# A fourth PSUM bank for the scores, and the attention outputs in halves of one bank

## The chip, the cores and the metric

The kernel runs on one core of a Trainium2 chip. The metric is the device time of one execution in microseconds (us). Engines are named as the profile names them: PE is TensorE (matmuls), PEld its weight loads, DVE is VectorE, ACT is ScalarE, POOL is GpSimd, and SP issues most DMAs. PSUM is the memory that PE writes its products to; here it is eight banks of 512 fp32 values in each of 128 partitions.

## The reference, cut to what matters

One layer with two attention branches over a prompt of 2048 frames (16 tiles of 128), and over 8 running streams of 16 frames each (one tile more, called the sample).

```python
h, gate = adaln_modulate(xp, c_prompt, norm_g[l], w_ada[l], b_ada[l])
qa, ka, va, za, qb, kb, vb, zb, ga, gb = project_inputs(h, w_in[l], pos_p)

def diff_attention(q, k, v, qpos, kpos, lam):          # branch a, 4 heads, each with two scores
    s = einsum('bqhcd,bkhcd->bhcqk', q, k) * HEAD_DIM_A ** -0.5
    p = softmax(where(mask, s, -inf), axis=-1)
    w = p[:, :, 0] - lam * p[:, :, 1]
    return einsum('bhqk,bkhe->bqhe', w, v)

def stick_breaking_attention(q, k, v, qpos, kpos):     # branch b, 8 heads
    z = einsum('bqhd,bkhd->bhqk', q, k) * HEAD_DIM_B ** -0.5
    log_1m = where(mask, log_sigmoid(-z), 0.0)
    log_a = log_sigmoid(z) + cumsum(log_1m, axis=3, reverse=True) - log_1m
    return einsum('bhqk,bkhd->bqhd', where(mask, exp(log_a), 0.0), v)

ya = (rms_norm(oa, subln_g) * (1 - lam_init) * silu(za)) @ w_branch_a
yb = (ob * silu(zb)) @ w_branch_b
xp = xp + gate * ((sigmoid(ga) * ya + sigmoid(gb) * yb) @ w_out)
```

The sample goes through the same with a cache of 512 older keys and values. Outputs are the normed results and the new keys and values.

## The kernel before, in words

There are three phases. In the first, the input is normed and modulated (`modulated`), tile group by tile group, and written as two fp16 halves (high and low part) to DRAM. The second is the longest: eight units, one after the other. An even unit (kind 0) is one head of the differential attention, an odd unit (kind 1) two heads of the stick-breaking attention. For each of its 17 tiles a unit projects queries, keys, values and gates (`project`, L452 for the main columns, L528 for gate columns, odd units only), transposes queries and keys (`transpose_qk`), forms scores (`scores`, L681 to L685), turns them into weights and multiplies these with the values (`pv_block`, L738 to L743). In the third phase the branch products (L1428) and the output product (L1457) run tile by tile, with the sample's attention beside them.

The way of one tile through the attention: a chunk of 512 scores is written to a bank called `s`. In an even unit DVE moves it out (L582), and the softmax follows later in pieces that are put off (`later_on`). In an odd unit ACT writes a sigmoid of it to SBUF and another one in place (both L128), and DVE then runs a product scan over the bank (L658); only after that scan is the bank free. POOL multiplies scan and sigmoid (L664). In both, the weights are cut into two fp16 halves (`turn`, L596, L597), transposed by a DMA (L604) into one of five buffers `wt`, and multiplied with the values by PE into a bank `o`. Tiles of more than 8 blocks of keys have two such segments for a head. After the last product of a tile its output is evicted (`natural`): by ACT alone in an even unit (L717), by ACT and then DVE in an odd one (L722, L723), with a product on POOL (L725); then it is stored (L732).

The eight banks of PSUM are given to four uses, for the whole kernel:

```python
BANKS = {"mm": 2, "s": 3, "t": 1, "o": 2}
```

`mm` takes projections and branch products, `t` transposes and gate columns, `s` scores, transposes of the last phase and small sums, `o` the attention's outputs and the last phase's output product. In the first phase `modulated` alternates between `s` and `o`.

The order of work is made in two steps. The program writes pieces of projection and of scores interleaved by their cost, and counts the cost in `spent`. Work that is put off lies in the list `due`, sorted by the value of `spent` at which it may go; the products of a segment are put there 27 units behind the transposing DMA (`PV_LAG`), and `give` takes everything out that is due. From this order a planner then fixes each engine's own order of instructions, with the waits that the use of tiles demands: an engine takes a later instruction where the planner holds an earlier one not to be ready.

Of the kernel before, what the change touches and what calls it, by code (L numbers as in the profile page):

```python
# [17 lines left out]
F32 = mybir.dt.float32  # L18
# [6 lines left out]
NOSYNC = mybir.DependencyInfo(mybir.DependencyClass.NoSync, mybir.DependencyReason.DATA)  # L25

P = 128
# [6 lines left out]
NT = SEQ // P  # L34
# [84 lines left out]
def layer_kernel(ctx: ExitStack, tc: tile.TileContext, a: dict):  # L119
# [61 lines left out]
    keys_d = {(n, h, i): dram.tile([P, 16, P], F16, name=f"keys_{n}{h}{i}") for n in ("ak", "bk") for h in range(4) for i in range(4)}  # L181

    con = ctx.enter_context(tc.tile_pool(name="con", bufs=1))
    ps = ctx.enter_context(tc.tile_pool(name="ps", bufs=2, space=bass.MemoryType.PSUM))
    tiny = ctx.enter_context(tc.tile_pool(name="tiny", bufs=6))
    unit = ctx.enter_context(tc.tile_pool(name="unit", bufs=2))
    c01 = ctx.enter_context(ExitStack())
# [8 lines left out]
    kvp = c01.enter_context(tc.tile_pool(name="kvp", bufs=2))  # L196
    stg = c01.enter_context(tc.tile_pool(name="stg", bufs=2))

    BANKS = {"mm": 2, "s": 3, "t": 1, "o": 2}

    def bank(tag, dt=F32):
        return ps.tile([P, 512 if dt == F32 else 1024], dt, tag=tag, name=f"ps_{tag}", bufs=BANKS[tag])


    ident = con.tile([P, P], F32, name="ident")
# [383 lines left out]
    def turn(job, seg, scale=None):  # L589

        nb = seg["hi"] - seg["lo"]
        nk = nb * P
        w16 = seg["n"].bitcast(F16)
        hi, lo, src = w16[:, 0:nk], w16[:, nk : 2 * nk], seg["p"][:, 0:nk]
        if scale is None:
            S.copy(out=hi, in_=src)  # L596
            V.tensor_tensor(out=lo, in0=src, in1=hi, op=ALU.subtract)  # L597
        else:
            split(hi, lo, src, scale, S)
        if job["t"] == NT:  # L600
            seg["wt"] = job["pool"].tile([P, 10, P], F16, tag="dwt", name="dwt", bufs=2)
        else:
            seg["wt"] = wtp.tile([P, 2 * SEG, P], F16, tag="wt", name="wt", bufs=WT_BUFS)
        nc.sync.dma_start_transpose(out=seg["wt"][:, 0 : 2 * nb, :], in_=w16[:, 0 : 2 * nk])  # L604
        if job["t"] < NT:
            cost = (PV_A, PV_B)[job["U"]["kind"]]
            for fn in pv(job, seg):
                later_on(PV_LAG, fn, cost)

    def softmax_pair(job):  # L610

# [55 lines left out]
    def scores(U, t, jobs):  # L667

        sc, kind = U["sc"], U["kind"]
        nch = t // 4 + 1  # L670
        own = [new_job(U, t, c, t + 1) for c in range(1 + kind)]
        jobs += own

        def chunk(c, ch):
            job = own[c if kind == 1 else 0]
            seg = job["segs"][ch * 4 // SEG]
            n = 512 if ch < t // 4 else (t % 4 + 1) * P
            p = bank("s")
            qst, kk = U["q", t], U["k"][ch]
            diag = ch == t // 4  # L680
            T.matmul(p[:, 0:n], qst[:, c, :], kk[:, c, 0:n], start=True, stop=False)  # L681
            T.matmul(p[:, 0:n], qst[:, 2 + c, :], kk[:, c, 0:n], start=False, stop=not diag)  # L682
            if diag:
                m = mask_a if kind == 0 else mask_b
                T.matmul(p[:, n - m.shape[1] : n], idb, m, start=False, stop=True)  # L685
            evacuate(job, seg, c, p, ch * 512 - seg["lo"] * P, n, sc[:, 3:4], sc[:, 4:5], ch)
            if kind == 0:
                if diag and c == 1:
                    softmax_pair(job)
                return  # L690
            i = job["segs"].index(seg)
            later = job["segs"][i + 1] if i + 1 < len(job["segs"]) else None
            stick(seg, later, ch * 512 - seg["lo"] * P, n, p)
            if ch * 4 == seg["lo"]:
                if later is not None:
                    stick_weights(job, later, None)
                if i == 0:
                    stick_weights(job, seg, later)

        def silu():  # L700

            z = silu_z[t % len(rings)]
            sg = stg.tile([P, 256], F32, tag="r2", name="r2", bufs=1)[:, 0:P]
            act(out=sg, in_=z, func=AF.Sigmoid)
            V.tensor_tensor(out=z, in0=z, in1=sg, op=ALU.mult)

        order = [(c, ch) for ch in range(nch) for c in range(2)] if kind == 0 else \
                [(c, ch) for c in range(2) for ch in reversed(range(nch))]
        return ([(0.1, silu)] if kind == 1 else []) + [(2.0 if ch < t // 4 else (t % 4 + 1) / 2, lambda c=c, ch=ch: chunk(c, ch)) for c, ch in order]
# [24 lines left out]
    def pv_block(job, seg, po, wj, vt, first, last):  # L734

        wt, nb, c = seg["wt"], seg["hi"] - seg["lo"], job["c"]
        if job["U"]["kind"] == 0:
            T.matmul(po[:, 0:P], wt[:, wj, :], vt[:, :, 0, :], start=first, stop=False)  # L738
            T.matmul(po[:, 0:P], wt[:, wj, :], vt[:, :, 1, :], start=False, stop=False)
            T.matmul(po[:, 0:P], wt[:, nb + wj, :], vt[:, :, 0, :], start=False, stop=last)  # L740
        else:
            T.matmul(po[:, c * P : (c + 1) * P], wt[:, wj, :], vt[:, c, :, :], start=first, stop=False)  # L742
            T.matmul(po[:, c * P : c * P + 64], wt[:, nb + wj, :], vt[:, c, 0, :], start=False, stop=last)  # L743

    due, spent = [], [0.0, 0]

    def later_on(lag, fn, cost=0.0):

        spent[1] += 1
        bisect.insort(due, (spent[0] + lag, spent[1], cost, fn))  # L750

    def pv(job, seg):

# [15 lines left out]
    def give(order, costs):  # L769

        for i, weight, fn in order:
            fn()
            spent[0] += weight * costs[i]
            while due and due[0][0] <= spent[0]:
                _, _, cost, product = due.pop(0)
                product()
                spent[0] += cost

    def cache_column(name, h):
        return "ab".index(name[0]) * 4 + h  # L780
# [231 lines left out]
    with tc.tile_pool(name="p0", bufs=1) as p0:  # L1012
# [160 lines left out]
        def modulated(g):  # L1173

            t0, w = GROUPS[g]
            nt = w // P
            box = {}

            def piece(k):
                if k == 0:  # L1180
                    box["hp"] = hp = hp_tile(F16)[:, 0 : nt * 2 * D].rearrange("p (i a k n) -> p i a k n", a=2, k=KT, n=P)
                    at_hand.update({t0 // P + i: hp[:, i, :, :, :] for i in range(nt)})
                hp = box["hp"]
                pt = bank("so"[k % 2])
                for i in range(nt):
                    T.matmul(pt[:, i * P : (i + 1) * P], xs[g][i][:, k * P : (k + 1) * P], diags[g][:, i, :], start=True, stop=True)
                tmp = p0.tile([P, 512], F32, tag="tmp", name="tmp", bufs=2)
                hi, lo = hp[:, :, 0, k, :], hp[:, :, 1, k, :]
                pv = pt[:, 0:w].rearrange("p (i n) -> p i n", n=P)
                tv = tmp[:, 0:w].rearrange("p (i n) -> p i n", n=P)  # L1190
                if t0 < SEQ:
                    S.activation(out=hi, in_=pv, func=AF.Identity, scale=ab[:, 0, k, 0:1], bias=ab[:, 1, k, 0:1])

                    S.activation(out=tv, in_=hi, func=AF.Identity, bias=minus_b[:, k : k + 1])
                    V.scalar_tensor_tensor(out=lo, in0=pv, scalar=ab[:, 0, k, 0:1], in1=tv, op0=ALU.mult, op1=ALU.subtract)
                else:
                    tb = tmp[:, 0:w].rearrange("p (b s) -> p b s", b=NB)
                    V.tensor_tensor(out=tb, in0=pt[:, 0:w].rearrange("p (b s) -> p b s", b=NB),
                                    in1=ab[:, 0, k, 1:9].unsqueeze(2).to_broadcast([P, NB, NS]), op=ALU.mult)
                    V.tensor_tensor(out=tb, in0=tb, in1=ab[:, 1, k, 1:9].unsqueeze(2).to_broadcast([P, NB, NS]), op=ALU.add)  # L1200
                    S.copy(out=hi, in_=tv)
                    G.tensor_tensor(out=lo, in0=tv, in1=hi, op=ALU.subtract)
                if k == KT - 1:
                    load(out=hT_d[g], in_=hp)

            return [(1.0, lambda k=k: piece(k)) for k in range(KT)]
# [144 lines left out]
    for n in range(len(steps) + 2):  # L1351
# [19 lines left out]
        if at[0] == len(line) and not pieces and not spare and not cached:  # L1371
            if cuts is None:
                cuts = early_work()
            pieces = [(1.0, fn) for fn in cuts[: -(-len(cuts) // (len(steps) + 2 - n))]]
            del cuts[: len(pieces)]
            if n == len(steps) + 1:
                while due and due[0][2] == 0.0:
                    due.pop(0)[3]()
                pieces += [(PV_B / PIECE, fn) for _, _, _, fn in due]
                due.clear()  # L1380
        give(interleaved(pieces, qk, side), (PIECE, CHUNK, 0.0))
    for _, _, _, fn in due:
        fn()
    c01.close()


    with ExitStack() as c2:
# [155 lines left out]
```

## Time and profile before

| | |
|---|---|
| median of 3 runs | 2275.9 us (2274.01 to 2279.74) |
| the profiled execution | 2280.78 us, span 2279.0 us |
| PE busy | 2086.9 us, 92% of the span |
| DVE busy | 1716.8 us, 75% |
| ACT busy | 1617.6 us, 71% |
| POOL busy | 701.4 us, 31% |
| mean granted clock of PE | 0.97 |

The span is the time from the first to the last instruction. The first phase ends near 140 us, the units' scores run from 140 to 1778 us, and the last phase follows. A row such as "PE ps_s L681 <- DVE sc_n L658: 31.3, 29, 3.0" says that PE's instructions of line 681, which write a bank `s`, waited 31.3 us in all for DVE's line 658, 29 times, 3.0 us at the longest. In a timeline a row gives start, duration, engine, line, operation and operands.

### The profile page before, as it was taken

The page shows a single profiled execution, that of the slowest core. Times are in us where ns is not written, and L with a number is a line of the kernel's source. Part 1 is how long each engine was busy: PE and PEld are TensorE (multiplying, and loading weights), DVE is VectorE, ACT ScalarE, POOL GpSimd, SP SyncE. Part 2 cuts the span into 40 slices and gives each one's busy share as a digit, 9 for nine tenths or more (in the row PEclk, how much of TensorE's full clock was granted, in tenths as well). Part 3 has the DMA queues.
Part 4 walks back from the last instruction along what each step waited for, and adds up shares of the span by engine and source line. Part 5 has one row for each costly group of instructions (what it writes and reads, how often), then busy time and mean ns, then how long its engine had stood idle before and what let it go on. Part 6 is the DMA issues. An engine that isn't in the chain of part 4 may idle for free. (4 is left out here: it accounts for less than half of the span.)

```text
span 2279.0 us, 41771 instructions
## 1 busy us (share of the span) xinstructions
PE 2086.9 (92%) x14752; PEld 1122.3 (49%) x14752; DVE 1716.8 (75%) x3795; ACT 1617.6 (71%) x3228; POOL 701.4 (31%) x610
## 2 busy tenths in 40 slices
PE   5998899999999899899999989998997789899998
PEld 3654455554555455455554545554553444444443
DVE  4658768778886787988688788877778777767753
ACT  3967777888887687888677788866778566556541
POOL 1223014446411444642044355302335212211211
PEclk8999999999999999999999999999998799999999
DMA  9777658998796999978888899655677899888321
GB/s 329 271 234 186 160 134 213 197 222 193 201 244 155 221 210 196 211 195 215 193 213 204 200 217 230 172 130 138 153 156 155 203 292 239 221 214 224 122 106 47
DMA packets 805827, 445.30 MB, mean 195 GB/s; under 512 B 537354, under 2 KB 744506, under 8 KB 805104
## 3 DMA queue, kind: packets, MB, share of 16 engines
q1 hardware_dynamic: 804668, 442.24, 78.5%
q8 instruction: 115, 1.88, 0.3%
q14 instruction: 96, 0.79, 0.1%
q10 hardware_dynamic: 948, 0.39, 0.1%
HBM read 228.82 MB, written 86.02 MB: 138 GB/s over the span
## 5 line engine op out<-in xcount | busy, mean ns | idle before, releaser
L664 POOL TENSOR_TENSOR sc_p<-sc_p,sc_n 128x127 f32<-128x127 f32 (+7 forms) x192 | 319.2, 1664 | 701.7 <-DVE sc_n L658 529.6
L452 PEld LDWEIGHTS <-hs 128*128 128x128 f16 x3120 | 293.4, 99 | 332.4 <-DMA hs<-hT_d 15.5
L452 PE MATMUL ps_mm<-wa,hs 128*128 128x512 f16 x1590 | 389.8, 384 | 9.5 <-DMA hs<-hT_d 8.6
L452 PE MATMUL ps_mm<-wb,hs 128*128 128x512 f16 x1530 | 376.9, 381 | 5.8 <-DMA hs<-hT_d 4.8
L528 PE MATMUL ps_t<-wb,hs 128*128 128x512 f16 x1224 | 290.7, 380 | 1.3 <-DVE qst L556 1.0
L658 DVE TENSOR_TENSOR_SCAN sc_n<-ps_s,sc_n,zero_t 128x512 f32<-128x512 f32 x192 | 245.4, 1278 | 48.9 <-ACT ps_s L128 44.2
L681 PE MATMUL ps_s<-k,qst 128*128 128x512 f16 (+3 forms) x640 | 226.0, 354 | 46.3 <-DVE sc_n L658 31.3
L597 DVE TENSOR_TENSOR sc_n<-sc_p,sc_n 128x128 f16<-128x128 f32 (+7 forms) x192 | 212.6, 1111 | 49.3 <-ACT sc_n L596 49.2
L128 ACT ACTIVATE sc_p<-ps_s,usc 128x512 f32<-128x512 f32 (+3 forms) x320 | 204.7, 640 | 61.5 <-PE ps_s L682 48.4
L528 PEld LDWEIGHTS <-hs 128*128 128x128 f16 x1632 | 156.5, 98 | 184.1 <-DVE qst L556 3.4
L682 PE MATMUL ps_s<-k,qst 128*128 128x512 f16 (+3 forms) x640 | 226.0, 354 | 0.0
L596 ACT CAST sc_n<-sc_p 128x128 f16<-128x128 f32 (+7 forms) x192 | 155.3, 814 | 68.6 <-POOL sc_p L664 68.0
L128 ACT ACTIVATE ps_s<-ps_s,usc 128x512 f32<-128x512 f32 (+3 forms) x328 | 199.6, 609 | 0.0
L1457 PE MATMUL ps_o<-wo,wb 128*128 128x512 f16 x816 | 182.9, 379 | 0.7 <-ACT wb L1266 0.7
L742 PE MATMUL ps_o<-v,wt 128*128 128x128 f16 x1088 | 131.4, 224 | 18.8 <-DMA wt<-sc_n 18.7
L582 DVE TENSOR_SCALAR_CACHE_REDUCE sc_n<-ps_s,usc 128x512 f32<-128x512 f32 (+3 forms) x160 | 106.4, 665 | 46.5 <-PE ps_s L685 30.8
L1457 PEld LDWEIGHTS <-wb 128*128 128x128 f16 x816 | 78.1, 98 | 94.5 <-issue 1.2
L738 PE MATMUL ps_o<-v,wt 128*128 128x128 f16 x544 | 100.4, 222 | 25.8 <-DMA wt<-sc_n 25.6
L743 PE MATMUL ps_o<-v,wt 128*128 128x64 f16 x1088 | 123.6, 197 | 0.0
L658 DVE TENSOR_TENSOR_SCAN sc_n<-ps_s,zero_t 128x128 f32<-128x128 f32 (+3 forms) x128 | 104.0, 813 | 25.5 <-ACT ps_s L128 24.9
L742 PEld LDWEIGHTS <-wt 128*128 128x128 f16 x1088 | 101.1, 101 | 44.2 <-DMA wt<-sc_n 24.8
L582 DVE TENSOR_SCALAR_CACHE_REDUCE sc_p<-ps_s,usc 128x512 f32<-128x512 f32 (+3 forms) x160 | 106.2, 664 | 21.3 <-PE ps_s L682 14.2
(369 smaller groups left out, 4425.7 us busy)
## 6 DMA issues: line engine op xcount, KB each, us to landing
hs<-hT_d SPq DMA_DIRECT2D x130, 512.0 KB, 4.4
g_d<-gt SPq DMA_DIRECT2D x68, 256.0 KB, 4.8
out_dram<-pr SPq DMA_DIRECT2D x204, 64.0 KB, 4.0
wa<-in_w_in_dram SPq DMA_DIRECT2D x34, 256.0 KB, 5.6
o_d<-o SPq DMA_DIRECT2D x136, 64.0 KB, 1.9
wa<-g_d SPq DMA_DIRECT2D x17, 512.0 KB, 5.5
wb<-g_d SPq DMA_DIRECT2D x17, 512.0 KB, 4.8
hs<-o_d SPq DMA_DIRECT2D x17, 512.0 KB, 5.5
```

The costliest lines, as they stand in the source:

```text
L128: i = S.activation(**kw)
L452: T.matmul(box["p"], box["h"][:, hi, k, :], U["w"][k][:, wi, :], start=(n == 0), stop=(n == 3 * KT - 1))
L528: T.matmul(box["g"][:, 0:gw], box["h"][:, hi, k, :], U["wg"][k // per][:, k % per, wi, :], start=(j == 0), stop=(j == 3 * KT - 1))
L582: V.tensor_scalar(out=dst[:, lo : lo + n], in0=p[:, 0:n], scalar1=sc_pos, scalar2=None, op0=ALU.mult, op1=ALU.max, accum_out=job["mx"][:, ...
L596: S.copy(out=hi, in_=src)
L597: V.tensor_tensor(out=lo, in0=src, in1=hi, op=ALU.subtract)
L658: V.tensor_tensor_scan(out=dst[:, lo : lo + n][:, ::-1], data0=src[:, 0:n][:, ::-1], data1=zero_t[:, 0:1].to_broadcast([P, n]), initial=fi ...
L664: G.tensor_tensor(out=p[:, 0:m], in0=p[:, 0:m], in1=n[:, 1 : m + 1], op=ALU.mult)
L681: T.matmul(p[:, 0:n], qst[:, c, :], kk[:, c, 0:n], start=True, stop=False)
L682: T.matmul(p[:, 0:n], qst[:, 2 + c, :], kk[:, c, 0:n], start=False, stop=not diag)
L742: T.matmul(po[:, c * P : (c + 1) * P], wt[:, wj, :], vt[:, c, :, :], start=first, stop=False)
L1457: T.matmul(po, st["y"][:, yi * 8 + k, :], wo[j * 4 + k // 2][:, wi, k % 2, :], start=(n == 0), stop=(n == 3 * KT - 1))
```

## The change

For the first two phases PSUM is split anew: two banks `mm`, four banks `s`, one bank `t`, and one bank that is a tile of its own and whose halves (columns 0 to 255 and 256 to 511) are the buffers `o` in turn. When the units are done, the pool is closed and another with the old split (2, 3, 1, 2) is opened for the last phase. In the first phase `modulated` uses `s` alone.

The products no longer lie in `due` but in a `queue` of segments, which is filled in the order of the tiles when their scores are planned. `give` takes products from the head of that queue alone, once it has them and their time has come. Beside that, the first product of an output is tied behind the last product of the output before it, on PE's own order, without a semaphore.

```diff
-    BANKS = {"mm": 2, "s": 3, "t": 1, "o": 2}
+    PHASE = {"mm": 2, "s": 3, "t": 1, "o": 2}
+    UNITS = {"mm": 2, "s": 4, "t": 1}
+    PARTS = {"o": [(0, 0, 256), (0, 256, 512)], "c": []}
+    ps = []
+
+    def banks(layout):
+        if ps:
+            ps[0].close()
+        stack = ctx.enter_context(ExitStack())
+        ps[:] = [stack, stack.enter_context(tc.tile_pool(name=f"ps{len(ps_names)}", bufs=2, space=bass.MemoryType.PSUM, reuse_waits="tile")), layout, {}]
+        ps_names.append(0)
+        if "o" not in layout:
+            fixed = [ps[1].tile([P, 512], F32, tag=f"fixed{i}", name=f"ps_fixed{i}", bufs=1) for i in range(8 - sum(layout.values()))]
+            ps[3] = {tag: [fixed[i][:, lo:hi] for i, lo, hi in parts] for tag, parts in PARTS.items()}
+
+    banks(UNITS)
 
     def bank(tag, dt=F32):
-        return ps.tile([P, 512 if dt == F32 else 1024], dt, tag=tag, name=f"ps_{tag}", bufs=BANKS[tag])
+        if tag in ps[3]:
+            ps[3][tag].append(ps[3][tag].pop(0))
+            return ps[3][tag][-1]
+        return ps[1].tile([P, 512 if dt == F32 else 1024], dt, tag=tag, name=f"ps_{tag}", bufs=ps[2][tag])
...
-            for fn in pv(job, seg):
-                later_on(PV_LAG, fn, cost)
+            seg["products"] = spent[0] + PV_LAG, cost, pv(job, seg)
...
         jobs += own
+        for job in own:
+            queue.extend(job["segs"] if kind == 0 else job["segs"][::-1])
...
+        if job["t"] < NT:
+            if first and groups:
+                tc.add_manual_dep(opens.ins, groups.pop().ins.name, NOSYNC, reason="one group at a time")
+            if last:
+                groups[:] = [ends]
...
             while due and due[0][0] <= spent[0]:
-                _, _, cost, product = due.pop(0)
-                product()
+                due.pop(0)[2]()
+            while queue and "products" in queue[0] and queue[0]["products"][0] <= spent[0]:
+                _, cost, products = queue[0]["products"]
+                products.pop(0)()
                 spent[0] += cost
+                if not products:
+                    queue.pop(0)
...
-                pt = bank("so"[k % 2])
+                pt = bank("s")
...
     c01.close()
+    banks(PHASE)
```

More of the change, by code (lines that the diff above doesn't have):

```diff
@@ L183, in layer_kernel @@
     con = ctx.enter_context(tc.tile_pool(name="con", bufs=1))
-    ps = ctx.enter_context(tc.tile_pool(name="ps", bufs=2, space=bass.MemoryType.PSUM))
     tiny = ctx.enter_context(tc.tile_pool(name="tiny", bufs=6))
@@ L197, in layer_kernel @@
     stg = c01.enter_context(tc.tile_pool(name="stg", bufs=2))
-    BANKS = {"mm": 2, "s": 3, "t": 1, "o": 2}
+    PHASE = {"mm": 2, "s": 3, "t": 1, "o": 2}
[11 more added lines that the diff above has]
+            ps[3] = {tag: [fixed[i][:, lo:hi] for i, lo, hi in parts] for tag, parts in PARTS.items()}
+    ps_names = []
+    banks(UNITS)
     def bank(tag, dt=F32):
-        return ps.tile([P, 512 if dt == F32 else 1024], dt, tag=tag, name=f"ps_{tag}", bufs=BANKS[tag])
+        if tag in ps[3]:
+            ps[3][tag].append(ps[3][tag].pop(0))
+            return ps[3][tag][-1]
+        return ps[1].tile([P, 512 if dt == F32 else 1024], dt, tag=tag, name=f"ps_{tag}", bufs=ps[2][tag])
     ident = con.tile([P, P], F32, name="ident")
@@ L737, in pv_block, with later_on @@
         if job["U"]["kind"] == 0:
-            T.matmul(po[:, 0:P], wt[:, wj, :], vt[:, :, 0, :], start=first, stop=False)
+            opens = T.matmul(po[:, 0:P], wt[:, wj, :], vt[:, :, 0, :], start=first, stop=False)
             T.matmul(po[:, 0:P], wt[:, wj, :], vt[:, :, 1, :], start=False, stop=False)
-            T.matmul(po[:, 0:P], wt[:, nb + wj, :], vt[:, :, 0, :], start=False, stop=last)
+            ends = T.matmul(po[:, 0:P], wt[:, nb + wj, :], vt[:, :, 0, :], start=False, stop=last)
         else:
-            T.matmul(po[:, c * P : (c + 1) * P], wt[:, wj, :], vt[:, c, :, :], start=first, stop=False)
-            T.matmul(po[:, c * P : c * P + 64], wt[:, nb + wj, :], vt[:, c, 0, :], start=False, stop=last)
+            opens = T.matmul(po[:, c * P : (c + 1) * P], wt[:, wj, :], vt[:, c, :, :], start=first, stop=False)
+            ends = T.matmul(po[:, c * P : c * P + 64], wt[:, nb + wj, :], vt[:, c, 0, :], start=False, stop=last)
+        if job["t"] < NT:
[3 more added lines that the diff above has]
+                groups[:] = [ends]
+    queue = []
+    groups = []
     due, spent = [], [0.0, 0]
-    def later_on(lag, fn, cost=0.0):
+    def later_on(lag, fn):
         spent[1] += 1
-        bisect.insort(due, (spent[0] + lag, spent[1], cost, fn))
+        bisect.insort(due, (spent[0] + lag, spent[1], fn))
     def pv(job, seg):
@@ L1376, in layer_kernel @@
             if n == len(steps) + 1:
-                while due and due[0][2] == 0.0:
-                    due.pop(0)[3]()
-                pieces += [(PV_B / PIECE, fn) for _, _, _, fn in due]
+                for _, _, fn in due:
+                    fn()
                 due.clear()
+                pieces += [(PV_B / PIECE, fn) for seg in queue for fn in seg["products"][2]]
+                queue.clear()
         give(interleaved(pieces, qk, side), (PIECE, CHUNK, 0.0))
-    for _, _, _, fn in due:
-        fn()
     c01.close()
+    banks(PHASE)
     with ExitStack() as c2:
```

## The prediction

> **What bounds the kernel now.** I read the page first, then the busy times by stage, TensorE's own waits over the whole span, and last the timelines around one output tile.
>
> ```profile
> span 2279.0 us, 41771 instructions
> PE 2086.9 (92%) x14752; PEld 1122.3 (49%) x14752; DVE 1716.8 (75%) x3795; ACT 1617.6 (71%) x3228; POOL 701.4 (31%) x610
> PE   5998899999999899899999989998997789899998
> PEclk8999999999999999999999999999998799999999
> ```
>
> TensorE (PE) is busy 92% of the span, so a shorter time has to come out of its 192 us of idle time (2279.0 - 2086.9), or out of the two slices where its clock dips. By stage (three of the four odd units, the stick-breaking ones; one even unit; then stretches of odd units):
>
> ```profile
> 315.00:545.00 230.00, 220.54 (x1586) 119.34 (x1585) 186.51 (x307) 183.04 (x379) 110.62 (x88) 0.99 0.89 202
> 1142.00:1377.00 235.00, 218.77 (x1524) 116.13 (x1522) 191.27 (x312) 182.74 (x377) 114.20 (x89) 0.99 0.92 210
> 1554.00:1778.00 224.00, 195.87 (x1407) 105.59 (x1406) 181.49 (x279) 163.10 (x325) 90.32 (x66) 0.93 0.70 151
> 965.00:1137.00 172.00, 165.53 (x1159) 90.91 (x1157) 136.57 (x389) 134.11 (x303) 41.13 (x45) 0.98 0.83 202
> 1142.00:1242.00 100.00, 92.77 (x639) 49.78 (x637) 82.26 (x168) 74.77 (x166) 45.17 (x39) 1.00 0.86 213
> 500.00:545.00 45.00, 39.24 (x308) 21.44 (x307) 43.56 (x49) 39.06 (x76) 32.81 (x25) 0.96 0.94 201
> 915.00:960.00 45.00, 38.93 (x309) 21.26 (x307) 40.58 (x43) 36.50 (x71) 29.44 (x23) 0.96 1.03 205
> 1320.00:1377.00 57.00, 48.00 (x348) 25.16 (x346) 48.10 (x53) 44.27 (x87) 36.92 (x29) 0.94 1.02 212
> 1720.00:1780.00 60.00, 38.24 (x323) 21.79 (x321) 54.95 (x64) 48.21 (x83) 33.94 (x19) 0.77 0.77 152
> ```
>
> After the stretch and its length stand PE, weight load, DVE, ACT and POOL, then the granted clock. PE bounds an even unit (165.5 of 172 us) and most of an odd one. At the end of an odd unit DVE takes over: 43.6 of 45 us, 40.6 of 45, 48.1 of 57, 55.0 of 60.
>
> What PE waits for, over the whole span (total, times, longest):
>
> ```profile
> PE ps_s L681 <- DVE sc_n L658: 31.3, 29, 3.0
> PE ps_o L738 <- DMA wt<-sc_n: 25.6, 13, 6.2
> PE ps_o L742 <- DMA wt<-sc_n: 18.7, 13, 4.8
> PE ps_mm L452 <- DMA hs<-hT_d: 13.4, 5, 4.8
> ...
> PE ps_s L681 <- DVE csc L924: 7.3, 7, 1.8
> PE ps_s L681 <- DVE sc_p L582: 3.9, 5, 2.5
> PE ps_s L225 <- DVE sc_n L658: 3.0, 3, 1.3
> PE ps_s L681 <- DVE sc_n L582: 2.4, 4, 1.5
> PE ps_s L681 <- DVE sc_q L233: 1.0, 1, 1.0
> PE ps_s L225 <- ACT junk L286: 0.5, 1, 0.5
> ```
>
> The six rows of ps_s are PE waiting for one of three scores banks: 49.4 us in 50 waits, 0.99 us each. No row has PE waiting for an eviction of ps_o: with two banks, an attention output never waits for its predecessor. So the change buys relief from 49.4 us with a buffer that now costs nothing.
>
> **Part 1, the fourth scores bank.** It can give back 49.4 us at most, and nothing if the scan behind the banks is what is slow. Where is it? The same query for four stretches, in this order: 1695 to 1792 us (the last unit's end), 500 to 545, 915 to 960, 1320 to 1377:
>
> ```profile
> PE ps_s L681 <- DVE sc_n L658: 12.0, 11, 2.7
> ...
> PE ps_s L681 <- DVE sc_n L658: 5.3, 5, 3.0
> ...
> PE ps_s L681 <- DVE sc_n L658: 3.7, 3, 2.9
> ...
> PE ps_s L681 <- DVE sc_n L658: 4.9, 4, 2.9
> ```
>
> In those stretches DVE is the busier engine, and a bank more only lets PE stand further ahead of it. I take these 25.9 us and the 1.0 us of sc_q, which falls at the same end, as not recovered. The other 22.5 us lie where DVE has room (82 of 100 us in the stretch 1142 to 1242) and a wait is 0.99 us long on the mean, which the head start of one more bank covers. Taken: -22 us; ends 0 and -49. Of other gains I count none.
>
> **Part 2, the outputs in halves of one bank.** Nothing is added on any engine; a wait may be. Around one output tile of an odd unit (PE's end of the tile, ACT's and DVE's eviction, PE's next tile):
>
> ```profile
> 1244.91 0.22 PE L742 MATMUL ps_o<-v,wt 128*128 128x128 f16 x1
> 1244.96 0.19 PE L743 MATMUL ps_o<-v,wt 128*128 128x64 f16 x1
> ...
> 1247.19 0.39 ACT L722 ACTIVATE ob<-ps_o,usc 128x128 f32<-128x128 f32 x1
> ...
> 1247.86 0.22 PE L742 MATMUL ps_o<-v,wt 128*128 128x128 f16 x1
> ...
> 1248.53 0.33 DVE L723 SCALAR_TENSOR_TENSOR o<-ps_o,usc,ob 128x128 f32<-128x128 f32 x1
> ```
>
> The tile ends at 1245.15; its eviction starts 2.0 us later and ends at 1248.86. PE has opened the next tile at 1247.86, 1.0 us before that, in the other bank. Sorted by their openings, 58 of the 127 successions look like this. The first and the last of them (PE's opening, then the eviction of the tile before):
>
> ```profile
> 158.36 0.22 PE L738 MATMUL ps_o<-v,wt 128*128 128x128 f16 x1
> 158.53 0.73 ACT L717 ACTIVATE o<-ps_o,usc 128x128 f32<-128x128 f32 x2
> ...
> 1777.75 0.29 PE L742 MATMUL ps_o<-v,wt 128*128 128x128 f16 x1 [3.78 <-DMA wt<-sc_n]
> 1781.51 0.34 DVE L723 SCALAR_TENSOR_TENSOR o<-ps_o,usc,ob 128x128 f32<-128x128 f32 x1
> ```
>
> Both halves are slices of one tile. If the wait goes by the slice, nothing changes: 0 us. If it goes by the whole bank, these 58 openings move behind the eviction. The order of instructions is planned, so PE will mostly be given projections first (L452, L528), and it stands still only where ACT or DVE comes later than planned; behind it on its queue then stand all projections and scores. The nearest row is the scores' own wait for a bank: about 1 us each time, 50 times in the 672 uses of a scores bank (640 chunks, 32 sums). If all 58 stalled: 58 x 0.99 = 57 us. At the scores' rate, doubled because nearly every one of these is tight: 58 x 2 x 50/672 x 0.99 = 8.5. Taken: +9 us, ends 0 and +57.
>
> The Trainium skill, page PSUM — Partial Sum Buffer, section "PSUM bank collisions raise a hardware error", says that two engines may not be on the same bank and quadrant at once, disjoint columns included. By this rule the halves are no double buffer and all 58 openings have to move; the trace of before cannot show it, since every output there has a bank of its own.
>
> **Part 3, products in the order of tiles.** Within a unit the order hardly changes. It changes where an odd unit follows an even one:
>
> ```profile
> 1157.09 0.22 PE L742 MATMUL ps_o<-v,wt 128*128 128x128 f16 x1
> ...
> 1160.34 0.22 PE L738 MATMUL ps_o<-v,wt 128*128 128x128 f16 x1
> ```
>
> Here the odd unit's first tile opens 3.3 us before the even unit's last; it will wait for the end of that one. No engine works more, but its wt buffers (two of five) are held longer, and on SP's queue the next transposes (L604), and behind them the loads of hs that L452 waits for, stand until one is freed. These waits exist already (44.3 us of wt and 13.4 us of hs in the rows above). There are four such changes of unit; if each costs two waits for wt of the mean 1.70 us (44.3/26), that is 14 us, and 0 if the slack holds. Taken: +3. The output's eviction and its store (L732) only move later; nothing waits for them before the last phase.
>
> **Part 4, the rest.** In the first phase the modulated tiles alternate over four banks where there were five:
>
> ```profile
> L1186 PE MATMUL ps_o<-diag,wide 128*128 128x128 f32 x104 | 15.3, 291 | 2.1 <-DVE tmp L1198 2.1
> ```
>
> This bank's row waits 2.1 us in all; a doubling is +2, taken +1. The last phase has its old split of the banks again: 0, hidden behind PE's other work while the last outputs leave, and the 2 us of two evictions if they do not.
>
> **Sum.** -22 + 9 + 3 + 1 = -9 us. The profiled execution took 2280.8 us for its span of 2279.0, 4.9 us above the median of the three runs, 2275.9. Applied to that execution the sum gives 2272, and on the median 2267.
>
> **Rivals.**
> - *The single output bank becomes the bound* (slower). Place: PE's opening matmul of a tile (L738, L742), waiting for L717 (even units) or L723 (odd ones). Price: up to 57 us; with three quarters of the 58 stalling, 43, and parts 1, 3 and 4 as above, 2276 - 22 + 4 + 43 = 2301. It decides once these waits pass 18 us, about one in three of the 58. For it: in odd units the eviction of most tiles ends several us after the last product, because ACT (183 of 235 us) and DVE (191) are well occupied. Against: even tiles have long gaps, and no such wait exists now. Chance 0.34. The skill's rule on collisions would work for this rival.
> - *The wait goes back to DVE.* The scores run one chunk further ahead, and PE meets the same scan one chunk later, as I assume for the ends of the units. Gain about 9 instead of 22, costs 13: 2280; with costs near 5, 2272. The change would then not do what it says. For it: DVE at 81% of odd units. Chance 0.24.
> - *More is gained than I count.* All 49.4 us go, and with the idle time the clock losses of three stretches: 45 x 0.04 + 45 x 0.04 + 57 x 0.06 = 7 us. 2275.9 - 49 - 7 + 13 = 2233. Against: DVE's 97% in 500 to 545. Chance 0.07.
>
> **How the numbers follow.** The forecast, 2267, has 0.35, with a range of its own from 2253 (no cost in part 2 and 3, slightly more gain) to 2269. A difference under 0.3%, 6.8 us, is about what a measurement of this kernel cannot tell from none; that is the second rival's 0.24. Faster is 0.35 + 0.07 = 0.42, slower 0.34. To hold 8 in 10 the range goes from 2246, which leaves out most of the third rival, to 2302, which leaves out the first one's upper part.
>
> **What would show it.** Right: the ps_s rows of PE's waits fall from 49 to about 27 us, what is left at the ends of odd units; a new row of ps_o waiting for o (L717, L723), near 9 us; rows of wt and hs within a few us; no opening of a tile ahead of the eviction before it. Wrong: new ps_o rows above 18 us, or rows of wt or hs grown by more than 10, or ps_s rows that stay above 40, or an odd unit's PE no busier than its 93%.

## The result, and the profile after

The changed kernel takes 2287.8 us (median of 6 runs, 2281.4 to 2292.5) against 2275.9 us before: a ratio of 1.0049, interval [1.0031, 1.0068]. On another chip it came to 1.0039 [1.0023, 1.0055]. It is slower by 9 to 11 us where 9 us faster were forecast. Below, the chips differ by a few us, so kernels are compared by their ratio to the kernel before on the same chip.

The page of the kernel after, span, busy times, PE's slices and its clock:

```profile
span 2289.1 us, 41834 instructions
PE 2090.8 (91%) x14752; PEld 1125.9 (49%) x14752; DVE 1745.1 (76%) x3795; ACT 1618.6 (71%) x3228; POOL 698.1 (30%) x610
PE   5998999999989999898999999998997689899998
PEclk7999999999999999999999999999999699999999
```

PE's work is the same. Of the 10.1 us more of span, 6.2 are more idle time (198.3 against 192.1) and 3.9 are longer busy time. What PE waits for in the kernel after, over the whole span (its score lines are L701 and L244, products L758 and L762 into the bank `ps_fixed`, projections L471, gate columns L547, transposes L560):

```profile
PE ps_mm L471 <- DMA hs<-hT_d: 23.3, 14, 2.5
PE ps_fixed L762 <- DMA wt<-sc_n: 21.1, 12, 4.3
PE ps_s L701 <- DVE sc_n L676: 17.2, 25, 2.5
PE ps_fixed L758 <- DMA wt<-sc_n: 13.9, 6, 4.5
PE ps_t L547 <- DVE qst L575: 9.2, 5, 3.2
...
PE ps_s L701 <- DVE sc_p L601: 7.5, 6, 3.6
PE ps_fixed L762 <- DVE o L743: 6.9, 3, 5.2
...
PE ps_t L560 <- ACT qst L575: 5.5, 1, 5.5
PE ps_t L560 <- DVE k L330: 5.4, 6, 0.9
...
PE ps_t L560 <- DVE sc_n L675: 2.5, 3, 0.8
PE ps_t L547 <- DVE col L314: 1.9, 2, 1.1
```

The same view of the kernel before, its largest rows of the bank t in the units:

```profile
PE ps_t L225 <- ACT gt L531: 1.8, 3, 1.0
PE ps_t L528 <- DVE qst L556: 1.7, 2, 1.0
PE ps_t L541 <- ACT qst L556: 1.6, 2, 0.9
```

With the small rows of the same kind, waits at the scores' lines fall from 49.4 to 29.6 us, as the fourth bank was meant to do. But waits at the units' lines that write the one bank t rise from 6.4 to 28.0 us; 5.4 of these are for the keys `k` that are transposed there, not for the bank. Waits for the single output bank come to 6.9 us, waits for wt fall from 44.3 to 35.0, and waits for hs rise from 13.4 to 23.3 us. Which part of the change moved which row is taken apart below (e2 and e1): most of the fall at the scores does not come from the fourth bank.

Where on the way the time is lost shows in the busy times from 1600 to 1700 us, in the last odd unit. First the kernel before, then the kernel after:

```profile
1600.00:1700.00 100.00, 99.67 (x670) 52.05 (x669) 74.44 (x116) 72.45 (x148) 37.48 (x30) 1.00 0.70 153
```

```profile
1600.00:1700.00 100.00, 89.38 (x586) 45.82 (x584) 65.23 (x100) 63.05 (x133) 30.68 (x26) 0.97 0.59 133
```

PE was full there and now idles 10.6 us, and executes 586 matmuls instead of 670. I also compared when each kernel had done the same share of PE's work, worked out from the start times of all matmuls. The kernel after is 8 us ahead at 310 us, at the end of the first unit, and still some 7 at 1380. At 1600 us it is level with the one before (+0.1 us), and at 1700 it is 15 us behind. It stays 12 to 20 us behind until 2000 us, and the last phase brings that down to 10.

What happens there, from the timelines of PE and SP. Before: the end of a tile's gate columns, the load of hs that follows at once, and the start of the next projection. Then the same three after:

```profile
1618.51 1.46 PE L528 MATMUL ps_t<-wb,hs 128*128 128x512 f16 x6
1620.00 0.33 SPq L429 DMA_DIRECT2D hs<-hT_d  x1
1622.13 0.60 PE L452 MATMUL ps_mm<-wb,hs 128*128 128x512 f16 x2
```

```profile
1611.56 1.89 PE L547 MATMUL ps_t<-wb,hs 128*128 128x512 f16 x8
1613.48 0.33 SPq L448 DMA_DIRECT2D hs<-hT_d  x1
1617.64 1.69 PE L471 MATMUL ps_mm<-wb,hs 128*128 128x512 f16 x6 [2.21 <-DMA hs<-hT_d]
```

In both, a load starts within 0.1 us of the end of the gate columns: these are the last readers of the hs buffer. Before, the projection that follows uses the load issued 12 us earlier, and does not wait. After, it waits for the very load that has just been issued, and starts 4.2 us behind it. The projections run one tile further ahead of the gate columns than before, so all three hs buffers are taken, and no load can be ahead. This can be counted in the start times. Take the last eight tiles of the last odd unit, and ask for each whether its projection starts before the gate columns of the tile two places earlier are done. In the kernel before none does, in the kernel after all eight do. From 1554 to 1800 us the waits come to:

```profile
PE ps_mm L471 <- DMA hs<-hT_d: 10.6, 6, 2.5
```

### The profile page after: what moved, and what is told of

Same layout as the page of the kernel before. It is cut to its first block, busy times and chain, and to the rows that moved or that the text cites. A ratio compares the mean times of both kernels' runs of the same rounds, so it can differ in the third digit from the quotient of the medians.

```text
span 2289.1 us, 41834 instructions
## 1 busy us (share of the span) xinstructions
PE 2090.8 (91%) x14752; PEld 1125.9 (49%) x14752; DVE 1745.1 (76%) x3795; ACT 1618.6 (71%) x3228; POOL 698.1 (30%) x610
## 5 line engine op out<-in xcount | busy, mean ns | idle before, releaser
L682 POOL TENSOR_TENSOR sc_p<-sc_p,sc_n 128x127 f32<-128x127 f32 (+7 forms) x192 | 308.6, 1610 | 584.5 <-DVE sc_n L676 536.3
L471 PEld LDWEIGHTS <-hs 128*128 128x128 f16 x3120 | 297.3, 99 | 358.0 <-DMA hs<-hT_d 27.9
L471 PE MATMUL ps_mm<-wb,hs 128*128 128x512 f16 x1530 | 371.5, 381 | 25.3 <-DMA hs<-hT_d 22.8
L471 PE MATMUL ps_mm<-wa,hs 128*128 128x512 f16 x1590 | 386.6, 383 | 0.5 <-DMA hs<-hT_d 0.5
L547 PE MATMUL ps_t<-wb,hs 128*128 128x512 f16 x1224 | 289.8, 382 | 6.0 <-DVE qst L575 4.9
L547 PEld LDWEIGHTS <-hs 128*128 128x128 f16 x1632 | 157.5, 99 | 197.0 <-DVE qst L575 12.5
L701 PE MATMUL ps_s<-k,qst 128*128 128x512 f16 (+3 forms) x640 | 223.9, 353 | 29.0 <-DVE sc_n L676 17.2
L616 DVE TENSOR_TENSOR sc_n<-sc_p,sc_n 128x128 f16<-128x128 f32 (+7 forms) x192 | 226.1, 1185 | 22.7 <-ACT sc_n L615 22.3
L762 PE MATMUL ps_fixed<-v,wt 128*128 128x128 f16 x1088 | 121.1, 226 | 28.0 <-DMA wt<-sc_n 21.1
L1496 POOL TENSOR_TENSOR x<-m,x 128x512 f32<-128x512 f32 x34 | 47.8, 1409 | 255.2 <-DVE m L1492 77.7
L762 PEld LDWEIGHTS <-wt 128*128 128x128 f16 x1088 | 101.3, 102 | 43.4 <-DMA wt<-sc_n 29.5
L512 POOL TENSOR_TENSOR rot<-pr,rope 128x256 f32<-128x256 f32 x68 | 58.2, 856 | 208.7 <-ACT pr L485 92.2
```

The source lines that it names most:

```text
L471: T.matmul(box["p"], box["h"][:, hi, k, :], U["w"][k][:, wi, :], start=(n == 0), stop=(n == 3 * KT - 1))
L547: T.matmul(box["g"][:, 0:gw], box["h"][:, hi, k, :], U["wg"][k // per][:, k % per, wi, :], start=(j == 0), stop=(j == 3 * KT - 1))
L682: G.tensor_tensor(out=p[:, 0:m], in0=p[:, 0:m], in1=n[:, 1 : m + 1], op=ALU.mult)
L762: opens = T.matmul(po[:, c * P : (c + 1) * P], wt[:, wj, :], vt[:, c, :, :], start=first, stop=False)
```

## The experiments

All are timed in five rounds beside the kernel before.

**The parts of the change, one at a time.**

```diff
# e1_three_s: the changed kernel, with
-    UNITS = {"mm": 2, "s": 4, "t": 1}
+    UNITS = {"mm": 2, "s": 3, "t": 1}
# e2_order_only: the changed kernel, with
-    UNITS = {"mm": 2, "s": 4, "t": 1}
-    PARTS = {"o": [(0, 0, 256), (0, 256, 512)], "c": []}
+    UNITS = {"mm": 2, "s": 3, "t": 1}
+    PARTS = {"o": [(0, 0, 512), (1, 0, 512)], "c": []}
```

> The changed kernel with three banks for the scores instead of four; the eighth bank lies idle, the outputs stay in one bank and in strict order. Theory A (the fourth bank does give about 10 to 20 us in the units, as the first five units of the changed kernel show, and the rest of the change takes more than that): slower than the changed kernel (2288) by 8 to 20 us, 2296 to 2308, and the waits of L701 for a scores bank back near 49 us. Theory B (the fourth bank gives nothing, the whole difference is the single output bank and a different order of work): within 4 us of 2288.

Measured: 1.0081 [1.0061, 1.0101]. Theory A in the time: the fourth bank is worth the step from 1.0081 to 1.0039 or 1.0049, 0.3 to 0.4%, 7 to 10 us, at the low end of the 8 to 20 that A put. Not in the waits: at the scores' lines they are 36.2 us (4.0 of them for queries), and not back near 49.

> The strict order of the products alone: three banks for the scores, two whole banks for the outputs as before. Theory A (strict order costs nothing, the single bank does): 2276, within 4 us of the kernel before, and no longer waits for hs in the last unit than before (4.8 us). Theory B (it is the strict order that makes the projections run ahead of the gate columns): 2284 to 2295, with about 10 us of waits for hs in the last unit.

Measured: 1.0020 [1.0008, 1.0031], 4.6 us. Theory A, but for a small cost of its own. That cost is not the order's alone: in this kernel the first phase also modulates over three banks instead of five, and the first scores start at 137.1 us instead of 132.8.

The row of the scores that wait for the scan, first of e2, then of e1; it has 31.3 us in the kernel before and 17.2 in the kernel after:

```profile
PE ps_s L701 <- DVE sc_n L676: 23.8, 22, 2.9
```

```profile
PE ps_s L701 <- DVE sc_n L676: 22.6, 24, 4.0
```

All waits at the scores' lines are 49.4 us before, 36.1 in e2, 36.2 in e1 and 29.6 in the changed kernel. Those at the lines that write the bank t are 6.4, 18.3, 20.5 and 28.0 us. So 13.3 of the 19.8 us that went at the scores, and 11.9 of the 21.6 us that came at t, are there in e2, with three scores banks and two output banks; the fourth bank takes 6.6 us at the scores and adds 7.5 at t.

The time, too, can be read from these two runs and the changed kernel. The step from two output banks to one, e2 to e1, costs 0.61% or 14 us. The waits for hs from 1554 to 1800 us, first of e1, then of e2:

```profile
PE ps_mm L471 <- DMA hs<-hT_d: 15.5, 8, 5.6
```

```profile
PE ps_mm L471 <- DMA hs<-hT_d: 5.2, 1, 5.2
```

With two output banks the hold on hs is not there (4.8 us in the kernel before); with one it is. Of the last eight tiles of that unit the projections run ahead, as counted above, for one in e2 and for all eight in e1.

**Where the freed bank goes.**

```diff
# e6_two_t:    +    UNITS = {"mm": 2, "s": 3, "t": 2}
# e7_three_mm: +    UNITS = {"mm": 3, "s": 3, "t": 1}
```

> The changed kernel with the freed bank given to the transposes and gate columns: three banks for the scores, two for t, outputs in one bank, strict order. In the changed kernel PE waits some 27 us for the bank t, against some 6 us before. Theory A (the single t bank takes over from the scores banks as what PE waits for, and holds the gate columns back): the t waits go, the waits for scores are back near 49 us, 2270 to 2285. Theory B (waits for banks are interchangeable, PE meets the slower engines anyway): 2283 to 2293.

Measured: 0.9999 [0.9986, 1.0011]; the time is A's. Against e1, where the bank is idle, a second bank t gives 0.8%, twice what a fourth scores bank gives. The waits are not quite A's: those at the lines that write t fall only from 20.5 to 17.8 us, because 12.2 of them are now for keys and queries that are not there yet (6.6 in e1), and those at the scores are 32.3 us. What goes is the hold: no projection of any odd unit runs ahead in the sense counted above, and the last unit has no wait for hs, where e1 has 15.5 us. From 1600 to 1700 us PE is full again:

```profile
1600.00:1700.00 100.00, 99.81 (x688) 52.58 (x687) 73.54 (x127) 71.25 (x147) 35.61 (x31) 1.00 0.72 156
```

> The changed kernel with the freed bank given to the projections: three banks mm, three for the scores, one t, outputs in one bank, strict order, three hs buffers. Theory A (in the last unit the projections already run too far ahead of the gate columns; a third mm bank lets them run further and holds hs longer): no better than with the bank idle, 1.006 to 1.012. Theory B (any bank more helps PE): 1.000 to 1.004.

Measured: 1.0146 [1.0130, 1.0162]. Slower than either theory put, and mostly not for the reason of theory A: the first unit's scores start 18 us later than in the kernel before (3 us in e1), so most of it is lost in the first phase, whose modulation uses the banks mm too. What there costs the time was not traced. From 1550 to 1700 us it loses 11 us, as e1 does. It does not tell the theories apart.

**Taking the hold on hs away.** A fourth hs buffer in the last unit, where weight buffers are spare:

```diff
+    ring, lent = list(hs), []
...
-        ahead[u, t] = hs[len(fetched) % 3].bitcast(F16)...
+        ring.append(ring.pop(0))
+        ahead[u, t] = ring[-1].bitcast(F16)...
...
                 free.extend(units[u - 1]["bufs"])
+            if u == 7:
+                lent.append(free.pop(0))
+                ring.insert(0, lent[0])
...
-            if u == 7 and not back and not spare and not cached and len(branch_weights) > 1:
+            if u == 7 and not back and not spare and not cached and len(branch_weights) > 2:
...
+        free.extend(lent)
         free.extend(units[7]["bufs"])
```

With a buffer lent, one branch weight is prepared later; the control below (e11) has the same. The first form took the buffers by a count modulo four; the last unit's sample tile then reads the next tile's input, so its rows come from other data.

> The changed kernel with a fourth buffer for the loaded input hs in the last unit only (a weight buffer lent to it; one of the branch weights is cut later for that). Theory A (in the last unit the projections run one tile further ahead of the gate columns, so all three hs buffers are held and PE waits 10.6 us for hs): these waits fall below 4 us, and the time by 8 to 15 us, to 2273 to 2280. Theory B (the waits for hs only stand in the place of others, the scores and the scan behind them set the pace): time within 4 us of 2288.

Measured: 0.9958 [0.9937, 0.9979]. With the buffers in the right turn, and with the control:

```diff
# after_again:        the changed kernel, nothing edited
# e10_four_hs:        the changed kernel, with the edit above
# e11_before_four_hs: the kernel before, with the edit above
```

> The changed kernel once more, on the chip of the three runs beside it, so that they can be compared there. 2283 to 2292, 0.3 to 0.7% above the kernel before.

> The changed kernel with a fourth hs buffer from the last unit on (a weight buffer lent, taken in turn with the other three; one branch weight is cut later). Theory A (all three hs buffers are held by gate columns that lag behind, PE waits for the load): the waits for hs in the last unit fall from 10.6 to below 3 us, and the time by 10 to 18 us, below the kernel before. Theory B (hs waits are a symptom, scores and scans set the pace): within 4 us of the changed kernel.

> The kernel before with the same fourth hs buffer. Theory A (the hold on hs comes with the single output bank; before, only one wait of 4.8 us is for hs in the last unit): 0 to 5 us faster than the kernel before. Theory B (a fourth hs buffer helps any order of this kernel): 10 us or more faster, as much as in the changed kernel.

Measured on one chip: the changed kernel 1.0039 [1.0023, 1.0055], with the fourth hs buffer 0.9953 [0.9936, 0.9969], the kernel before with it 0.9993 [0.9979, 1.0008]. Theory A in both: the buffer is worth 0.86%, or 20 us, to the changed kernel and nothing that can be told to the one before. From 1554 to 1800 us e10 has no wait for hs, although its projections run as far ahead as in the changed kernel, for all of the last eight tiles. The same three moments in the kernel with the fourth hs buffer (e10), the projection now ahead of the load that follows the gate columns:

```profile
1616.13 1.46 PE L549 MATMUL ps_t<-wb,hs 128*128 128x512 f16 x6
1617.62 0.32 SPq L450 DMA_DIRECT2D hs<-hT_d  x1
1619.74 1.46 PE L473 MATMUL ps_mm<-wb,hs 128*128 128x512 f16 x6
```

The projection starts 2.1 us after that load is issued and waits for none. PE from 1600 to 1700 us in e10:

```profile
1600.00:1700.00 100.00, 98.46 (x684) 52.03 (x682) 75.67 (x112) 71.77 (x148) 38.51 (x29) 1.00 0.66 146
```

e10 is the fastest kernel of the study, 11 us below the kernel before.

**The prices once the hold is gone.** The same edit on e6, e1 and e2:

```diff
# e12_two_t_four_hs:    e6 with the fourth hs buffer
# e13_three_s_four_hs:  e1 with the fourth hs buffer
# e14_order_four_hs:    e2 with the fourth hs buffer
```

> Single output bank, strict order, three banks for the scores, two for t, and the fourth hs buffer in the last unit. Theory A (the gate columns lag because t and the outputs have one bank each; a second t bank already removes the waits for hs in the last unit, so the fourth hs buffer has nothing left to remove): within 5 us of the kernel with two t banks and three hs buffers, ratio 0.998 to 1.002 to the kernel before. Theory B (the second t bank and the fourth hs buffer help in different places): the two gains add up, ratio 0.988 to 0.994.

Measured: 0.9982 [0.9968, 0.9996]. Theory A: where a second bank t has removed the waits for hs, the buffer finds 0.17%, which is within the noise of the two, and not 0.86%.

> Single output bank, strict order, three banks for the scores, one for t, and the fourth hs buffer in the last unit: against the changed kernel with the fourth hs buffer (0.9953) it prices the fourth scores bank without the hold on hs. Theory A (the fourth scores bank is worth about 7 us, as with three hs buffers, 1.0081 against 1.004 to 1.005): 0.998 to 1.000. Theory B (with the hold gone the whole 22 us of the prediction appear): 1.004 to 1.006.

Measured: 0.9995 [0.9983, 1.0006]. Theory A: against e10 the fourth scores bank is worth 0.42%, 10 us; the 22 us of the prediction do not appear. Against e1 the fourth hs buffer is worth 0.86%, as it is with four scores banks.

> Strict order, two output banks, three banks for the scores, one for t, and the fourth hs buffer in the last unit: against the same with a single output bank it prices the single bank without the hold on hs. Theory A (most of the 14 us that the single output bank cost with three hs buffers was the hold): within 4 us of the kernel with the single bank and the fourth hs buffer, and, as with the kernel before, no gain from that buffer: 1.000 to 1.003. Theory B (the waits for evictions and the later products are the cost): 8 us or more faster than the single bank.

Measured: 1.0019 [1.0006, 1.0033]. Theory A: the buffer changes nothing here, and with the hold gone the kernel with a single output bank (e13, 0.9995) is no slower than the one with two; it is even 0.24% faster, a little more than the 4 us that A allowed. The whole 14 us of e1 against e2 were the hold on hs.

**What a scores bank is worth.**

```diff
# e8_two_s: the kernel before, with
-    BANKS = {"mm": 2, "s": 3, "t": 1, "o": 2}
+    BANKS = {"mm": 2, "s": 2, "t": 1, "o": 2}
```

> The kernel before with two banks for the scores instead of three, the eighth bank idle: what a scores bank is worth. If the wait for scores banks sets the pace, 49 us of waits grow by more than as much again and the kernel is 40 us slower or more. If DVE's scan behind the banks sets it, 10 to 25 us slower. If the third to fourth bank was worth 7 us, as the runs with three and four in the changed kernel say, the second to third should be worth more than that.

Measured: 1.0881 [1.0859, 1.0904], 201 us. The three largest of PE's waits in it:

```profile
PE ps_s L681 <- DVE sc_n L658: 54.7, 48, 4.0
PE ps_o L742 <- DMA wt<-sc_n: 53.9, 46, 3.8
PE ps_mm L452 <- DMA hs<-hT_d: 36.2, 23, 5.5
```

Of the cases expected it is the first, 40 us or more, by far. Two banks are far too few, and of the two steps the third bank is nearly everything: 201 us for the third, 7 to 10 for the fourth. Only a part of the loss stands at the scores: their waits rise by 44 us, those for wt by 37 and those for hs by 23. That late scores make late weights and late products, which hold wt and hs, is the likely reason, and was not traced. The projections run ahead here too, for all of the last eight tiles of the last unit and in the earlier odd units as well, although there are two output banks; in that unit the waits for hs stay at 4.1 us all the same. The wait rows of one resource understate what it is worth.

## Why the prediction was wrong

*Part 2, the single output bank: the waits right, the consequence missed; this is the step that gave the time its wrong sign.* The eviction waits were put at 9 us and are 6.9. None of the 127 openings comes ahead of the end of the eviction before it, where 58 did; so the case "by the whole bank" of the prediction holds. The Trainium skill, page PSUM — Partial Sum Buffer, section "PSUM bank collisions raise a hardware error", has the rule that two engines may not be on the same bank and quadrant at once. The trace agrees with it, with 0 of 127. The order is kept by waits of the program, as the row of L762 for L743 shows; what the chip would do without them no run here shows. The step that failed is the sentence that PE "will mostly be given projections first", counted as cover at no cost. The projections were given, and each that is drawn ahead holds an hs buffer until its gate columns have run. That cost 14 us net (e2 to e1). The hold itself costs 20 us, which a fourth hs buffer gives back with three scores banks (e1 to e13) and with four (the changed kernel to e10 on its chip).

*Part 1, the fourth scores bank: mis-sized, and half right by luck.* The waits at the scores' lines fell by 19.8 us, near the 22 counted, but 13.3 of that came with the order of the products and the first phase (e2), where the time rose by 4.6 us. The fourth bank itself took 6.6 us of them (e1 to after) and added 7.5 at the bank t, a single buffer whose rows I had not priced because they were small. The term of -22 came out at -7 to -10 (e1 against after, e13 against e10). Its step counted a wait removed as time won. The rows do not account for what was won either; 2.3 us of it, and 5.1 from e13 to e10, are an earlier start of the first scores, so lie in the first phase. Most of the rest is won in the first unit: at 310 us the changed kernel is 8 us ahead of the kernel before, and e1 is 2. The second rival named a return of the waits, but put it at the scan. A small slip: the rows of ps_s that the prediction adds up are seven, not six; the sum of 49.4 is right.

*The slower rival* gave the right sign and the wrong mechanism: its point of decision, 18 us of waits at the opening of an output tile, was not reached (6.9 us). The cost lay at the load of the projections' input, a place that this rival does not name.

*Part 3, the order: near in size.* Forecast +3 us, measured +4.6 (e2) and +4.3 (e14, 0.19%), with the narrower first phase in both, so the order has no price of its own. It named the loads of hs, but tied them to SP's queue behind the transposes; in the last odd unit the load in fact waited for its buffer. That waits would move from the scores to t with it, as in e2, was not foreseen.

*Part 4* stays within what these runs can tell: the first scores start 0.7 us later in the changed kernel and 2.0 us later in e11, whose first phase is that of the kernel before.

The measured terms add up: +4.6 (order and first phase) +14 (single output bank) -7 to -10 (fourth bank) gives +9 to +12 us, and +9 to +11 were measured. Most of the signs that the prediction named for being right were there all the same: 29.6 us at the scores (27 forecast), 6.9 at the output bank (9), and no opening ahead of an eviction. The rows of hs grew by 9.9 us, just short of the 10 that would have counted against it.

What stays open: why the planner draws the projections ahead in the last odd unit of the kernel after more than in the earlier ones (11 of 14 tiles, against 4 or 5). Of the kernels made from the changed one, only those with one output bank, one bank t and three hs buffers lose there; undoing any one of the three (e2, e6, e10) removes it. How the order comes about was not traced further, nor why the 7 us of lead at 1380 us are gone by 1600.

## What to carry to other kernels

When a buffer is taken from one stage, ask not only who will wait for it, but what the engine does instead: work drawn ahead pins its own inputs, and the loss can appear at a load that has nothing to do with the buffer. A wait removed is not time won: here the order of the products took 13 us of waits from the scores, and the kernel became slower. A count of the resource, one less and one more, prices it better than its wait rows. When several things change at once, take them apart before saying which of them moved a row. Two halves of one PSUM bank worked here as one buffer: 0 of 127 outputs were opened before the eviction of the one before.

## What the runs showed of the hardware that was not expected

The granted clock was lower where PE was idle more. From 1600 to 1700 us it was 1.00 in the kernel before, with PE busy 99.67 us, and 0.97 in the kernel after, with 89.38 us. With two scores banks (e8) it is 0.944 over the run, and PE is busy 2162.1 us for the same 14752 matmuls that take 2086.9 us at 0.970 in the kernel before:

```profile
PE 2162.1 (87%) x14752; PEld 1145.3 (46%) x14752; DVE 1715.6 (69%) x3795; ACT 1627.7 (66%) x3228; POOL 670.0 (27%) x610
```

So 75 us of that kernel's loss are not idle time but longer busy time, in a kernel whose waits are none longer than 6 us in the rows shown. An estimate: in proportion to the clock, 2086.9 us at 0.970 would be 2144 at 0.944, which is 57 of the 75 us; what the rest is stays open. That the short waits lower the clock is not shown, since no run changes them alone.
